# A residual added by TensorE: identity products into the sums' banks, last products by tokens, and squares and last scaling read from PSUM

## The chip, the cores and the metric

One core of a Trainium2 chip runs the whole layer as one program. The metric is the device time in microseconds, the median of several executions. The engines are TensorE (PE: products, with its weight loads as PEld), VectorE (DVE), ScalarE (ACT), GpSimd (POOL) and SyncE (SP), which issues most of the DMAs.

## The reference, cut to what matters

The input x has 256 tokens of 1024 columns, float32. After two attention mixers, x has been raised by the mixers' output; what follows is the part that the change touches:

```python
    x = x + mixed @ w_out[l]
    h = rmsnorm(x, g_ffn[l])
    x = x + conv_ffn(h, w_up[l], conv_w[l], conv_b[l], w_down[l])
return rmsnorm(x, g_final)          # y * rsqrt(mean(y*y) + 1e-6) * g_final

def conv_ffn(h, w_up, conv_w, conv_b, w_down):
    u, gate = jnp.split(h @ w_up, 2, axis=-1)        # 1024 -> 2816 each
    ...                                              # causal conv of width 3 over tokens: uc
    return (jax.nn.gelu(uc) * gate) @ w_down         # 2816 -> 1024
```

## The kernel before, in words

Weights come in units of 128 x 2048 values: one DMA each into `raw`, then ACT makes the high half `whi` (L128) and DVE the low half `wlo` (L132). A product of float32 quality is three products of such halves (high by high, high by low, low by high); the halves are of a type (float32r) that TensorE takes as one record per product. The units are run through in one loop (L1094), in a fixed order. Each engine executes its own instructions in the order in which the program writes them, and a wait holds up all that is behind it on that engine.

From `NFIRST` on the loop does the feed-forward part. For each of 11 steps j there are two units for `w_up` (256 columns each, sums in PSUM tiles `ps_d` and `ps_o` in turn) and, two steps later, one for `w_down` (`mm_down_part`, L630). The down products keep tokens as the 128 output partitions: the sums are `ffn["y"][t][ch]`, with t the half of the tokens and ch the half of the columns, four banks of 128 x 512: both halves of t = 0 in one tile `ps_s`, those of t = 1 in two tiles `ps_t`. They add up over all 11 steps; the last two steps (NF - 2 and NF - 1) are not run in the loop but by `last`, one block of the output at a time, so that the final norm can begin while others are still summed.

Up to there the residual x is kept transposed (`xT`, columns on partitions), since that is how the mixers leave it. In the loop's round `NFIRST + 1` 16 transposes (L1161) by `ident`, the 128 x 128 identity, bring it into the order of tokens, through `ps_t` and `ps_s`, and four ACT copies (L1164) take it to `X` in SBUF. Just ahead of them `rows_of` (L222) spreads the norm's factors over the partitions by two plain float32 products with `ident`.

`last(t, ch, c0, c1)` runs the 24 (or, for half the columns, 12) products of the last two steps for a block, adds the sums to X on DVE (L1201), takes squares and their sum on ACT (L1206), adds the sum to the running one on POOL (L1207), and multiplies X by `gf`, the final norm's gain, on DVE (L1210). The last quarter takes its squares on DVE (L1203). When both column halves of a t are done, POOL takes the power -0.5 (L1209). `store` scales by it on ACT (L1218), for t = 1 partly on DVE (L1216), and issues the DMA out. The order of the blocks is (0,0), (1,0), (0,1), (1,1) in two quarters of 256 columns; the second of these quarters sums its last two steps in a bank of its own, from `ps_d`, and its earlier steps are added to X at the very beginning (L1222).

Of the kernel before, what the change touches and what calls it, by code (L numbers as in the profile page):

```python
# [14 lines left out]
AF = mybir.ActivationFunctionType  # L15
OP = mybir.AluOpType
# [3 lines left out]
D = 1024  # L20
DFF = 2816
NF = DFF // 256
# [71 lines left out]
def build(ctx, tc, a, out):  # L94
    nc = tc.nc
    V, A, P, T = nc.vector, nc.scalar, nc.gpsimd, nc.tensor
# [7 lines left out]
    def pd(shape, tag="d"):  # L104
        return ps.tile([128] + shape, F32, name="ps_" + tag, tag=tag, bufs=1 if tag == "s" else 2)

    xT = const.tile([128, 8, S], F32, name="xT")
# [3 lines left out]
    ident = const.tile([128, 128], F32, name="ident")  # L111
# [5 lines left out]
    nhalf, inv_d, epsc = cst[:, 0:2], cst[:, 2:3], cst[:, 3:4]  # L117
# [66 lines left out]
    def w3(u, k):  # L184
        n = u.n // k
        return (u.hi[:, u.o:u.o + u.n].rearrange("p (k c) -> p k c", k=k),
                u.lo[:, u.o:u.o + u.n].rearrange("p (k c) -> p k c", k=k))
# [386 lines left out]
    ffn = {}  # L574
# [44 lines left out]
    def mm_down_part(u, j, tcs, c0=0, c1=512, own=None):  # L619

        wh, wl = w3(u, 2)
        h, l = ffn["a", j]
        half = [(0, 256), (256, 512)] if c1 - c0 == 512 else [(c0, c1)]
        start, seen = j == (0 if own is None else NF - 2), set()
        for n, (w, x) in enumerate(((wh, h), (wh, l), (wl, h))):
            for t in sorted({t for t, _ in tcs}):
                for kt in range(2):
                    for ch in [ch for q, ch in tcs if q == t]:
                        for b, e in half:
                            T.matmul(ffn["y"][t][ch][:, b:e] if own is None else own, x[:, kt, t * 128:t * 128 + 128],  # L630
                                     w[:, kt, ch * 512 + b:ch * 512 + e], start=start and (t, ch) not in seen,
                                     stop=j == NF - 1 and n == 2 and kt == 1, skip_group_check=True)
                            seen.add((t, ch))

    def mm_down(j):
        def f(u):
            if j == 0:
                s2 = pd([2, 512], "s")
                ta = pd([512], "t")
                tb = pd([512], "t")  # L640
                ffn["y"] = [[s2[:, 0], s2[:, 1]], [ta, tb]]
            if j < NF - 2:
                mm_down_part(u, j, [(t, ch) for t in range(2) for ch in range(2)])
        return f
# [15 lines left out]
    downs = [Unit(2048, mm_down(j)) for j in range(NF)]  # L660
# [353 lines left out]
    def load_to(n):  # L1014
        nonlocal loaded
        while loaded < min(n, len(units)):
            load_unit(units[loaded])
            loaded += 1
# [4 lines left out]
    for n, f in zip(CHUNKS, first):  # L1023
        w = f.shape[-1]
# [32 lines left out]
    for n in CHUNKS:  # L1057
# [6 lines left out]
        for v, u in enumerate((u0, u1)):  # L1064
            r = f[:, :, 256 + 256 * v:512 + 256 * v]
# [24 lines left out]
    def at(i):  # L1090
        return items.get(i, [])

    post = []
    for i, u in enumerate(units):  # L1094
        load_to(i + LA)
        if i == 9:
            cmp_sum()
        for it in at(i - 3):
            it.fin()
        for it in at(i - 2):  # L1100
            it.te()
        for it in at(i - 1):
            it.sm()
        if i == 10:
            cmp_gelu()
        if i == 2:
            hi_of(3)
            lo_of(3)
        if i == 9:
            for it in at(i - 1):  # L1110
                it.sm2()
        if i > 2:
            lo_of(i + 1)
        if i != 9:
            for it in at(i - 1):
                it.sm2()
        if i == 14:
            nc.sync.dma_start(xT, a["xT"])
        if i == 3:
            hi_of(5)  # L1120
            mixer_tiles()
            xc_tile()
            split_cmp(0)
            split_cmp(1)
            u1.evac(u1)
        if i == 4:
            split_keys()
        if i == 11:
            cmp_kv_ev()
        if i == 14:  # L1130

            ob = att.tile([128, 4, S], F32R, name="ob", tag="qa")
            OB.update(h=ob[:, 0:2], l=ob[:, 2:4])
        if i in (23, 24):
            m = ML[i - 23]
            A.activation(m, m, AF.Sigmoid)
        if i == NFIRST:
            st.close()
            ffn["pool"] = ctx.enter_context(tc.tile_pool(name="ffn", bufs=1))
            gf = ffn["pool"].tile([128, D], F32, name="gf")  # L1140
            nc.scalar.dma_start(gf, bass.AP(tensor=a["g_final"].tensor, offset=a["g_final"].offset,
                                            ap=[[0, 128], [1, D]]))
            X = ffn["pool"].tile([128, 2, D], F32, name="X")
            sq = ffn["pool"].tile([128, 512], F32, name="sq")
        if 24 <= i <= 25:
            hi_of(i + 2)
        if i in (24, NFIRST + 2):
            rt["kick"] = "own"
        u.mm(u)
        if not 24 <= i <= 26 and i > 1 and i != 3:  # L1150
            hi_of(i + 2)
        if i == 2:
            u0.evac(u0)
        if i == NFIRST + 1:
            rt["R2"] = rows_of(rt["rs2"], "R2", "o")
            units[NFIRST].evac(units[NFIRST])
            ps2 = pd([2, 512], "s")
            pt = [pd([512], "t"), pd([512], "t"), ps2[:, 0], ps2[:, 1]]
            for q in range(4):
                for c in range(4):  # L1160
                    T.transpose(pt[q][:, c * 128:c * 128 + 128], xT[:, 4 * (q % 2) + c, q // 2 * 128:q // 2 * 128 + 128],  # L1161
                                ident)
            for q in range(4):
                A.activation(X[:, q // 2, q % 2 * 512:q % 2 * 512 + 512], pt[q], AF.Copy)  # L1164
        if post:
            post.pop()()
        if u.pre:
            u.pre(u)
        if u.evac and i not in (0, 1, NFIRST):
            u.evac(u)  # L1170
        if i in (6, 7):
            q_parts(i - 6)
        if i == 7:
            gates_of()
        if u.pre:
            post.append(post_g(len([q for q in units[:i] if q.pre])))
        for it in at(i - 2):
            it.pv()
        for it in at(i - 1):
            it.tr()  # L1180
        for it in at(i):
            it.qk()
        if i == 9:
            cmp_fold()
        if i == 10:
            cmp_kv()


    ss3, rs3 = tiny[:, 6:11], tiny[:, 11:13]

    def last(t, ch, c0=0, c1=512):

        xs, y = X[:, t, ch * 512 + c0:ch * 512 + c1], ffn["y"][t][ch][:, c0:c1]
        w = c1 - c0
        if c0:
            y = pd([512])[:, :w]
        for j in (NF - 2, NF - 1):
            mm_down_part(downs[j], j, [(t, ch)], c0, c1, y if c0 else None)
        n = {(0, 0): 0, (1, 0): 1, (0, 1): 2, (1, 1): 3}[t, ch] + (c0 > 0)
        ss, r = ss3[:, n:n + 1], rs3[:, t:t + 1]  # L1200
        V.tensor_tensor(out=xs, in0=xs, in1=y, op=OP.add)  # L1201
        if c0:
            V.tensor_tensor_reduce(out=sq[:, w:2 * w], in0=xs, in1=xs, scale=1.0 / D, scalar=r,  # L1203
                                   op0=OP.mult, op1=OP.add, accum_out=ss)
        else:
            A.activation(sq[:, :w], xs, AF.Square, scale=1.0 / 32, accum_out=ss)  # L1206
            P.tensor_tensor(out=r, in0=r if ch else epsc, in1=ss, op=OP.add)  # L1207
        if ch and (c0 or t == 0):
            P.tensor_tensor(out=r, in0=ss if c0 else r, in1=nhalf[:, 0:1], op=OP.pow)  # L1209
        V.tensor_tensor(out=xs, in0=xs, in1=gf[:, ch * 512 + c0:ch * 512 + c1], op=OP.mult)  # L1210

    def store(t, c):

        o, r = out[0, t * 128:(t + 1) * 128], rs3[:, t:t + 1]
        if c < D:
            V.tensor_scalar(X[:, t, c:], X[:, t, c:], r, None, op0=OP.mult)  # L1216
            nc.sync.dma_start(o[:, c:], X[:, t, c:])
        A.activation(X[:, t, :c], X[:, t, :c], AF.Copy, scale=r)  # L1218
        (nc.scalar if t else nc.sync).dma_start(o[:, :c], X[:, t, :c])

    x = X[:, 1, 768:1024]
    V.tensor_tensor(out=x, in0=x, in1=ffn["y"][1][1][:, 256:512], op=OP.add)  # L1222
    last(0, 0)
    last(1, 0)
    last(0, 1)
    last(1, 1, 0, 256)
    store(0, D)
    last(1, 1, 256, 512)
    store(1, 384)


# [18 lines left out]
```

## Time and profile before

| | us |
|---|---|
| median of 3 runs (406.04 to 407.66) | 406.07 |
| the profiled execution | 406.5 |
| its span | 404.7 |
| TensorE busy in it | 394.7 |
| DVE busy | 291.2 |
| ACT busy | 212.4 |
| POOL busy | 31.2 |

The times of rows below are counted from the start of the profiled span. A row of the timeline has the start, the duration of the group, engine, line and operation, what is written from what, and the count. A bracket at its end is the idle time of the engine just before, and what ended it. Ends of products are modelled; their starts are not.

### The profile page before, as it was taken

The page shows a single profiled execution, that of the slowest core. Times are in us where ns is not written, and L with a number is a line of the kernel's source. Part 1 is how long each engine was busy: PE and PEld are TensorE (multiplying, and loading weights), DVE is VectorE, ACT ScalarE, POOL GpSimd, SP SyncE. Part 2 cuts the span into 40 slices and gives each one's busy share as a digit, 9 for nine tenths or more (in the row PEclk, how much of TensorE's full clock was granted, in tenths as well). Part 3 has the DMA queues.
Part 4 walks back from the last instruction along what each step waited for, and adds up shares of the span by engine and source line. Part 5 has one row for each costly group of instructions (what it writes and reads, how often), then busy time and mean ns, then how long its engine had stood idle before and what let it go on. Part 6 is the DMA issues. An engine that isn't in the chain of part 4 may idle for free.

```text
span 404.7 us, 8015 instructions
## 1 busy us (share of the span) xinstructions
PE 394.7 (98%) x3412; PEld 383.2 (95%) x3412; DVE 291.2 (72%) x486; ACT 212.4 (52%) x293; POOL 31.2 (8%) x58
## 2 busy tenths in 40 slices
PE   8999989999999999999999999999999999999993
PEld 6999989999998989999999999999999999999992
DVE  5879889887786557458897499676594774946853
ACT  5776764366664345663554765445264352643512
POOL 7100000000000000061143000000000000000012
PEclk9999999999999999999999999999999999999997
DMA  8965746345332532343556346662734726438002
GB/s 319 390 251 207 249 168 209 105 158 220 144 105 105 201 113 105 131 181 108 206 208 235 130 136 236 255 222 108 296 119 194 266 99 261 160 152 299 15 0 105
DMA packets 10980, 72.59 MB, mean 179 GB/s; under 512 B 1216, under 2 KB 1472, under 8 KB 2880
## 3 DMA queue, kind: packets, MB, share of 16 engines
q1 hardware_dynamic: 10512, 70.96, 48.2%
q10 hardware_dynamic: 432, 1.11, 0.7%
q8 instruction: 27, 0.44, 0.4%
q14 instruction: 9, 0.07, 0.1%
HBM read 71.02 MB, written 1.05 MB: 178 GB/s over the span
## 4 chain that ended last, share of the span: by engine, by line
PE 83%; DVE 10%; ACT 2%; DMA 2%; issue 1%; SPq 0%; POOLq 0%; POOL 0%; ACTq 0%
PE ps_d L177 25%; PE ps_d L182 12%; PE ps_o L177 9%; PE ps_s L630 8%; PE ps_t L630 7%; PE ps_o L182 5%; DVE wlo L132 4%; DMA first<-in_first_dram 2%; PE ps_t L177 2%; DVE hTl L202 2%; PE ps_d L344 2%; PE ps_o L905 2%; PE ps_s L946 1%; PE ps_t L892 1%; PE ps_d L280 1%
## 5 line engine op out<-in xcount | busy, mean ns | idle before, releaser
L132 DVE TENSOR_TENSOR wlo<-raw,whi 128x2048 fp32r<-128x2048 f32 (+2 forms) x61 | 135.2, 2217 | 4.2 <-ACT whi L128 4.2
L128 ACT ACTIVATE whi<-raw 128x2048 fp32r<-128x2048 f32 (+1 forms) x61 | 114.8, 1883 | 33.6 <-DMA raw<-in_wts_dram 28.8
L177 PE MATMUL ps_d<-hTh,whi 128*128 128x256 f32 x384 | 90.1, 280 | 0.0
L177 PE MATMUL ps_d<-hTl,whi 128*128 128x256 f32 x384 | 89.0, 277 | 0.0
L177 PEld LDWEIGHTS ps_d<-hTh,whi 128*128 128x128 f32 x384 | 72.2, 188 | 1.7 <-issue 1.3
L177 PEld LDWEIGHTS ps_d<-hTl,whi 128*128 128x128 f32 x384 | 72.2, 188 | 0.0
L182 PE MATMUL ps_d<-hTh,wlo 128*128 128x256 f32 x384 | 47.8, 277 | 0.0
L182 PEld LDWEIGHTS ps_d<-hTh,wlo 128*128 128x128 f32 x384 | 45.7, 188 | 0.0
L177 PE MATMUL ps_o<-hTh,whi 128*128 128x256 f32 x160 | 36.9, 277 | 0.0
L177 PE MATMUL ps_o<-hTl,whi 128*128 128x256 f32 x160 | 36.8, 276 | 0.0
L585 ACT ACTIVATE C<-U,small 128x256 f32<-128x256 f32 x22 | 12.0, 595 | 44.1 <-DVE U L581 44.1
L177 PEld LDWEIGHTS ps_o<-hTl,whi 128*128 128x128 f32 x160 | 30.1, 188 | 0.0
L177 PEld LDWEIGHTS ps_o<-hTh,whi 128*128 128x128 f32 x160 | 30.0, 188 | 0.0
L589 DVE SCALAR_TENSOR_TENSOR C<-U,small,C 128x256 f32<-128x256 f32 x44 | 19.4, 482 | 7.5 <-ACT C L585 7.4
L869 ACT ACTIVATE E<-E,ast 128x256 f32<-128x256 f32 (+1 forms) x32 | 14.2, 444 | 13.4 <-DVE ast L864 13.4
L581 DVE TENSOR_TENSOR U<-ps_d,R 128x512 f32<-128x512 f32 x6 | 4.1, 690 | 23.0 <-PE ps_d L182 19.2
L182 PE MATMUL ps_o<-hTh,wlo 128*128 128x256 f32 x160 | 19.8, 276 | 0.0
L132 POOL TENSOR_TENSOR wlo<-raw,whi 128x1024 fp32r<-128x1024 f32 x3 | 7.7, 2579 | 154.8 <-ACT whi L128 154.8
L182 PEld LDWEIGHTS ps_o<-hTh,wlo 128*128 128x128 f32 x160 | 18.9, 188 | 0.0
L581 DVE TENSOR_TENSOR U<-ps_o,R 128x512 f32<-128x512 f32 x5 | 3.4, 689 | 17.6 <-PE ps_o L182 17.6
L1207 POOL TENSOR_TENSOR tiny<-cst,tiny 128x1 f32<-128x1 f32 x2 | 1.4, 696 | 170.6 <-ACT sq L1206 170.6
L366 DVE TENSOR_TENSOR ML<-ps_d,R 128x512 f32<-128x512 f32 x8 | 5.5, 692 | 12.3 <-PE ps_d L182 12.3
(269 smaller groups left out, 762.5 us busy)
## 6 DMA issues: line engine op xcount, KB each, us to landing
raw<-in_wts_dram SPq DMA_DIRECT2D x61, 1024.0 KB, 4.8
first<-in_first_dram SPq DMA_DIRECT2D x2, 768.0 KB, 8.1
raw<-in_wts_dram SPq DMA_DIRECT2D x1, 1120.0 KB, 11.0
xn<-in_xn_dram SPq DMA_DIRECT2D x2, 512.0 KB, 12.4
xT<-in_xT_dram SPq DMA_DIRECT2D x1, 1024.0 KB, 6.9
first<-in_first_dram SPq DMA_DIRECT2D x2, 384.0 KB, 5.3
gf<-in_g_final_dram ACTq DMA_DIRECT2D x1, 512.0 KB, 3.7
out_dram<-X SPq DMA_DIRECT2D x1, 512.0 KB, 2.6
```

The costliest lines, as they stand in the source:

```text
L128: A.activation(u.hi[:, u.o + c0:u.o + c1], u.raw[:, c0:c1], AF.Copy)
L132: (eng or V).tensor_sub(u.lo[:, u.o + c0:u.o + c1], u.raw[:, c0:c1], u.hi.bitcast(F32)[:, u.o + c0:u.o + c1])
L177: T.matmul(po, l, r, start=start and bank not in banks, stop=False, skip_group_check=True)
L182: T.matmul(po, l, r, start=False, stop=stop and n == len(ks) - 1, skip_group_check=True)
L202: V.scalar_tensor_tensor(hTl[:, kt], x, g[:, kt:kt + 1], hTh.bitcast(F32)[:, kt], op0=OP.mult, op1=OP.subtract)
L344: T.matmul(u.p[:, i], l[:, kt, i * 128:i * 128 + 128], r[:, kt], start=kt == 0 and i == 0 and q == 0, stop=kt == 7 and q == 2, skip_group_ ...
L581: V.tensor_tensor(out=U[:, :, 2:], in0=u.p, in1=bc(rt["R2"], 2), op=OP.mult)
L585: A.activation(C[:, c], U[:, c, 2:], AF.Identity, scale=CW(2, t), bias=CB[:, t:t + 1])
L589: V.scalar_tensor_tensor(C[:, c], U[:, c, w:w + S], CW(w, t), C[:, c], op0=OP.mult, op1=OP.add)
L630: T.matmul(ffn["y"][t][ch][:, b:e] if own is None else own, x[:, kt, t * 128:t * 128 + 128], w[:, kt, ch * 512 + b:ch * 512 + e], start=st ...
L869: A.activation(self.E[:, i], self.E[:, i], AF.Exp, bias=mn[:, i:i + 1], scale=-1.0, accum_out=dn[:, i:i + 1])
L905: T.matmul(oA[js[c]][g * 64:g * 64 + 64, t * 128:(t + 1) * 128], Vn[:, k, b * 128 + g * 64:b * 128 + g * 64 + 64], self.PT[:, i], start=t ...
```

## The change

The four banks of the sums are now taken in round `NFIRST + 1`, and instead of 16 transposes 16 plain float32 products of the tiles of `xT` with `ident` write the residual into them: the first of each bank clears it, the other three write their own columns. All down products then add to it, and the four ACT copies into X go away. `last` goes by tokens: (0,0), (0,1), then the scaling and the store of t = 0, then (1,0) and the two quarters of (1,1). ACT takes the squares directly from the bank, DVE multiplies bank by `gf` into X. Now the first quarter of (1,1) has the bank of its own: its earlier sums are copied to X by ACT at the beginning (L1208 of the changed kernel), and DVE adds. For the last quarter ACT takes the squares from the bank, DVE adds their sum to the running one (L1201), POOL takes the power, and one DVE instruction multiplies bank, factor and `gf` (L1217). ACT scales 512 columns of t = 1 and DVE 256 more, which are 512 with those of L1217; each half has its store.

```diff
-        start, seen = j == (0 if own is None else NF - 2), set()
+        start, seen = own is not None and j == NF - 2, set()
...
         if i == NFIRST + 1:
             rt["R2"] = rows_of(rt["rs2"], "R2", "o")
             units[NFIRST].evac(units[NFIRST])
-            ps2 = pd([2, 512], "s")
-            pt = [pd([512], "t"), pd([512], "t"), ps2[:, 0], ps2[:, 1]]
-            for q in range(4):
-                for c in range(4):
-                    T.transpose(pt[q][:, c * 128:c * 128 + 128], xT[:, 4 * (q % 2) + c, q // 2 * 128:q // 2 * 128 + 128],
-                                ident)
-            for q in range(4):
-                A.activation(X[:, q // 2, q % 2 * 512:q % 2 * 512 + 512], pt[q], AF.Copy)
+
+            s2 = pd([2, 512], "s")
+            ta = pd([512], "t")
+            tb = pd([512], "t")
+            ffn["y"] = [[s2[:, 0], s2[:, 1]], [ta, tb]]
+            for t in range(2):
+                for ch in range(2):
+                    for c in range(4):
+                        T.matmul(ffn["y"][t][ch][:, c * 128:c * 128 + 128], xT[:, 4 * ch + c, t * 128:t * 128 + 128],
+                                 ident, start=c == 0, stop=False, skip_group_check=True)
...
-        if c0:
-            y = pd([512])[:, :w]
+        own = pd([512])[:, :w] if c1 == 256 else None
         for j in (NF - 2, NF - 1):
-            mm_down_part(downs[j], j, [(t, ch)], c0, c1, y if c0 else None)
+            mm_down_part(downs[j], j, [(t, ch)], c0, c1, own)
         n = {(0, 0): 0, (1, 0): 1, (0, 1): 2, (1, 1): 3}[t, ch] + (c0 > 0)
         ss, r = ss3[:, n:n + 1], rs3[:, t:t + 1]
-        V.tensor_tensor(out=xs, in0=xs, in1=y, op=OP.add)
-        if c0:
-            V.tensor_tensor_reduce(out=sq[:, w:2 * w], in0=xs, in1=xs, scale=1.0 / D, scalar=r,
-                                   op0=OP.mult, op1=OP.add, accum_out=ss)
-        else:
-            A.activation(sq[:, :w], xs, AF.Square, scale=1.0 / 32, accum_out=ss)
-            P.tensor_tensor(out=r, in0=r if ch else epsc, in1=ss, op=OP.add)
+        if own is not None:
+            V.tensor_tensor(out=xs, in0=xs, in1=own, op=OP.add)
+            y = xs
+        A.activation(sq[:, :w], y, AF.Square, scale=1.0 / 32, accum_out=ss)
+        (V if c0 else P).tensor_tensor(out=r, in0=r if ch else epsc, in1=ss, op=OP.add)
         if ch and (c0 or t == 0):
-            P.tensor_tensor(out=r, in0=ss if c0 else r, in1=nhalf[:, 0:1], op=OP.pow)
-        V.tensor_tensor(out=xs, in0=xs, in1=gf[:, ch * 512 + c0:ch * 512 + c1], op=OP.mult)
...
+            P.tensor_tensor(out=r, in0=r, in1=nhalf[:, 0:1], op=OP.pow)
+        if not c0:
+            V.tensor_tensor(out=xs, in0=y, in1=gf[:, ch * 512 + c0:ch * 512 + c1], op=OP.mult)
+
+
+    A.activation(X[:, 1, 512:768], ffn["y"][1][1][:, 0:256], AF.Copy)
     last(0, 0)
+    last(0, 1)
+    A.activation(X[:, 0], X[:, 0], AF.Copy, scale=rs3[:, 0:1])
+    nc.sync.dma_start(out[0, 0:128], X[:, 0])
     last(1, 0)
-    last(0, 1)
     last(1, 1, 0, 256)
-    store(0, D)
     last(1, 1, 256, 512)
-    store(1, 384)
+    o, r = out[0, 128:256], rs3[:, 1:2]
+    V.scalar_tensor_tensor(X[:, 1, 768:], ffn["y"][1][1][:, 256:512], r, gf[:, 768:], op0=OP.mult, op1=OP.mult)
+    V.tensor_scalar(X[:, 1, 512:768], X[:, 1, 512:768], r, None, op0=OP.mult)
+    nc.sync.dma_start(o[:, 512:], X[:, 1, 512:])
+    A.activation(X[:, 1, :512], X[:, 1, :512], AF.Copy, scale=r)
+    nc.scalar.dma_start(o[:, :512], X[:, 1, :512])
```

How this moves the instructions is seen best on the two engines that take turns behind the last products. On ACT, from the first squares to the end of the program, there stood before (`sq,tiny<-X` are squares and their sum, `X<-X,tiny` a scaling by the norm's factor):

```order
L1206 ACTIVATE sq,tiny<-X 128x512 [waits DVE_49]
L1206 ACTIVATE sq,tiny<-X 128x512 [waits DVE_49,Activation_49] x2
L1206 ACTIVATE sq,tiny<-X 128x256 [waits DVE_49,Activation_49]
L1218 ACTIVATE X<-X,tiny 128x1024 [waits Pool_49]
L1218 ACTIVATE X<-X,tiny 128x384 [waits Pool_49]
L1219 DMA out_dram<-X 128x384 [waits Activation_49]
```

And in the changed kernel, on the same engine and in the same place:

```order
L1208 ACTIVATE X<-ps_t 128x256 [waits PE_49]
L1200 ACTIVATE sq,tiny<-ps_s 128x512 [waits PE_49]
L1200 ACTIVATE sq,tiny<-ps_s 128x512 [waits DVE_49,PE_49]
L1211 ACTIVATE X<-X,tiny 128x1024 [waits DVE_49,Pool_49]
L1200 ACTIVATE sq,tiny<-ps_t 128x512 [waits PE_49,Activation_49]
L1200 ACTIVATE sq,tiny<-X 128x256 [waits DVE_49,Activation_49]
L1200 ACTIVATE sq,tiny<-ps_t 128x256 [waits PE_49,Activation_49]
L1220 ACTIVATE X<-X,tiny 128x512 [waits Pool_49]
```

The squares wait for TensorE instead of DVE, the scaling of 1024 columns has moved from behind all of ACT's squares to between those of t = 0 and those of t = 1, and the last quarter's squares are ACT's. On DVE, the same stretch before (`X<-X,ps_s` is the addition of sums to X, `X<-X,gf` the product with the gain; the two rows of ISA are squares with their sum and the read of that sum):

```order
L1222 TENSOR_TENSOR X<-X,ps_t 128x256 [waits PE_49]
L1201 TENSOR_TENSOR X<-X,ps_s 128x512 [waits PE_49]
...
L1210 TENSOR_TENSOR X<-X,gf 128x512 [waits Activation_49]
L1201 TENSOR_TENSOR X<-X,ps_t 128x256 [waits PE_49]
L1210 TENSOR_TENSOR X<-X,gf 128x256 [waits Activation_49]
L1201 TENSOR_TENSOR X<-X,ps_d 128x256 [waits PE_49]
L1203 ISA sq,tiny<-X,tiny 128x256 [waits DVE_49,Pool_49]
L1203 ISA tiny 128x1
L1210 TENSOR_TENSOR X<-X,gf 128x256 [waits DVE_49]
L1216 TENSOR_SCALAR X<-X,tiny 128x640 [waits DVE_49,Pool_49]
```

And in the changed kernel:

```order
L1205 TENSOR_TENSOR X<-ps_s,gf 128x512 [waits Activation_49] x2
L1205 TENSOR_TENSOR X<-ps_t,gf 128x512 [waits Activation_49]
L1198 TENSOR_TENSOR X<-X,ps_d 128x256 [waits PE_49]
L1205 TENSOR_TENSOR X<-X,gf 128x256 [waits Activation_49]
L1201 TENSOR_TENSOR tiny<-tiny 128x1 [waits Activation_49,Pool_49]
L1217 SCALAR_TENSOR_TENSOR X<-ps_t,tiny,gf 128x256 [waits Pool_49]
L1218 TENSOR_SCALAR X<-X,tiny 128x256 [waits DVE_49]
```

Four of five additions of sums are gone from DVE, the products with the gain read the banks and wait for ACT's squares of the same bank, and what is left for DVE behind the last product is the addition of one column ahead of POOL's power, and two instructions behind it.

## Rows read from the trace of the kernel before

**Rows 1.** Busy time by stretch: start:end, its length, then busy of each engine (instructions).

```profile
core 0: us, PE busy (x) PEld busy (x) DVE busy (x) ACT busy (x) POOL busy (x), PEclk, DMA share, GB/s
...
300.00:350.00 50.00, 50.00 (x437) 50.00 (x437) 33.24 (x37) 23.36 (x21) 0.00 (x0) 1.00 0.53 194
```

**Rows 2.** Waits from 216 us on: who, for whom, total, times, longest.

```profile
PEld ps_d L280 <- DVE wlo L132: 0.6, 1, 0.6
```

**Rows 3.** Timeline of the weight loads: start, duration, line, operation, stationary size, count.

```profile
65.23 0.85 PEld L905 LDWEIGHTS ps_o<-PT,Vn 128*64 128x64 f32 x16
...
223.95 0.53 PEld L222 LDWEIGHTS ps_o<-ident,tiny 128*128 128x128 f32 x4
224.40 0.91 PEld L1161 LDWEIGHTS ps_t<-ident,xT 128*128 128x128 f32 x8
...
226.15 0.19 PEld L172 LDWEIGHTS ps_o<-hTh,whi 128*128 128x128 f32 x1
```

**Rows 4.** Groups by line and shape, TensorE: shape, count, busy us, mean ns.

```profile
L222 PE MATMUL ps_o<-ident,tiny 128*128 128x128 f32 x8 | 1.2, 274 | 0.0
```

**Rows 5.** The chain that ended last, at the last down products: start, duration, what.

```profile
392.05 2.84 PE ps_s L630 x24
...
394.92 0.70 DVE X L1201
```

**Rows 6.** Timeline of all engines from the last quarter's products to the last store.

```profile
396.56 0.63 POOL L1207 TENSOR_TENSOR tiny<-tiny 128x1 f32<-128x1 f32 x1 [2.20 <-ACT sq L1206]
...
397.28 0.55 POOL L1209 TENSOR_TENSOR tiny<-tiny,cst 128x1 f32<-128x1 f32 x1
397.31 0.40 PE L630 MATMUL ps_d<-wlo,ah 128*128 128x256 f32 x2
397.57 0.42 ACT L1206 ACTIVATE sq<-X 128x256 f32<-128x256 f32 x1 [1.15 <-DVE X L1201]
397.89 0.19 ACT L1206 ACTIVATION_READ_ACCUMULATOR sq<-X 128x1 f32 x1
397.99 1.13 ACT L1218 ACTIVATE X<-X,tiny 128x1024 f32<-128x1024 f32 x1
398.11 0.42 DVE L1210 TENSOR_TENSOR X<-X,gf 128x256 f32<-128x256 f32 x1 [0.64 <-ACT sq L1206]
...
398.45 0.41 DVE L1201 TENSOR_TENSOR X<-X,ps_d 128x256 f32<-128x256 f32 x1
399.02 0.48 DVE L1203 CUSTOM_DVE_ANT_0 sq<-X,tiny 128x256 f32<-128x256 f32 x1 [0.15 <-DVE X L1201]
...
399.59 0.79 POOL L1209 TENSOR_TENSOR tiny<-tiny,cst 128x1 f32<-128x1 f32 x1 [1.00 <-DVE tiny L1203]
400.41 0.61 ACT L1218 ACTIVATE X<-X,tiny 128x384 f32<-128x384 f32 x1 [1.29 <-POOL tiny L1209]
...
401.06 0.36 ACTq L1219 DMA_DIRECT2D out_dram<-X  x1
```

**Rows 7.** Groups by line and shape, ACT and DVE: count, busy us, mean ns.

```profile
L1164 ACT ACTIVATE X<-ps_s 128x512 f32<-128x512 f32 x2 | 1.1, 595 | 0.0
L917 ACT ACTIVATE oah<-ps_o 128x256 fp32r<-128x256 f32 x4 | 1.3, 381 | 4.3 <-PE ps_o L910 4.3
...
L1210 DVE TENSOR_TENSOR X<-X,gf 128x512 f32<-128x512 f32 x3 | 2.1, 693 | 2.5 <-ACT sq L1206 2.5
L964 DVE TENSOR_SCALAR ast<-ast 128x1 f32<-128x1 f32 x4 | 0.6, 147 | 0.0
L454 DVE SCALAR_TENSOR_TENSOR qb<-ps_d,scB,R 128x256 f32<-128x256 f32 x6 | 2.6, 479 | 1.0 <-PE ps_d L182 1.0
L883 DVE TENSOR_SCALAR E<-E,ast 128x256 f32<-128x256 f32 x16 | 4.6, 350 | 0.1
```

**Rows 8.** The last two stores: DMA issues by line with size and us to landing.

```profile
out_dram<-X SPq DMA_DIRECT2D x1, 320.0 KB, 2.4
out_dram<-X ACTq DMA_DIRECT2D x1, 192.0 KB, 2.6
```

More of the change, by code (lines that the diff above doesn't have):

```diff
@@ L636, in f @@
         def f(u):
[L637 to L641, printed above, removed]
             if j < NF - 2:
@@ L1208, in last @@
-        if ch and (c0 or t == 0):
-            P.tensor_tensor(out=r, in0=ss if c0 else r, in1=nhalf[:, 0:1], op=OP.pow)
-        V.tensor_tensor(out=xs, in0=xs, in1=gf[:, ch * 512 + c0:ch * 512 + c1], op=OP.mult)
[L1212 to L1219, printed above, removed]
@@ L1221, in build @@
-    x = X[:, 1, 768:1024]
-    V.tensor_tensor(out=x, in0=x, in1=ffn["y"][1][1][:, 256:512], op=OP.add)
+        if own is not None:
[3 more added lines that the diff above has]
+        (V if c0 else P).tensor_tensor(out=r, in0=r if ch else epsc, in1=ss, op=OP.add)
+        if ch and (c0 or t == 0):
+            P.tensor_tensor(out=r, in0=r, in1=nhalf[:, 0:1], op=OP.pow)
+        if not c0:
+            V.tensor_tensor(out=xs, in0=y, in1=gf[:, ch * 512 + c0:ch * 512 + c1], op=OP.mult)
```

## The prediction

> **What bounds the kernel now.** I read first the busy time by stretch, then the waits, then the weight loads around the removed transposes, and last the end of the program row by row. In the stretch from 300 to 350 us TensorE is busy for 50.00 of 50.00 us and its weight loads too, at a granted clock of 1.00, which is the 2.4 GHz level, while DVE has 33.24 and ACT 23.36 [rows 1]. From 216 us to the end the only thing that TensorE's queue waits for is one low half of a weight, 0.6 us [rows 2], and that is before the transposes. They run from 224.40 to 226.15 us, closed in by weight loads on both sides without a gap [rows 3]. So from there to its last product TensorE sets the time: what is added to it moves the end by as much, and what is taken from DVE or ACT in that part moves nothing. After the last product, which ends at 397.31 + 0.40 = 397.71 us [rows 6], a chain over DVE, POOL and ACT sets the end. I call this moment E. The two ends are separate sums, since nothing that TensorE does after E matters and nothing of the last chain begins before the last products do.
>
> **The identity products.** The change puts 16 products of xT with the identity, float32 on both sides, where 16 transposes of the same tiles stood. The 16 transposes (eight into one tile, eight more into the next) took 226.15 - 224.40 = 1.75 us [rows 3], 0.109 us each. A float32 product is not one record but two: the program's two row-spreading products just before give 4 records (it calls that helper twice with two products, and the trace has 8 in all [rows 4]), and those 4 took 224.40 - 223.95 = 0.45 us [rows 3], so 0.225 us a product. They have the same shape, 128x128 stationary and 128 columns of the identity moving. 16 x 0.225 = 3.60 us, so TensorE gets 3.60 - 1.75 = **1.85 us** longer. Bounds: the products with only 64 stationary columns and the same 128 moving ones took 0.85 us for 16 records, 0.053 each [rows 3]; if that were the pace, 32 records would be 1.70 us and the change -0.05. At the pace of the down products, 2.84 us for 24 [rows 5], 0.118 each, 32 records are 3.79 and the change +2.04. I take 1.85, since its row has both sizes right and the lower one has half of the weight columns.
>
> The Trainium skill (TensorE: Matmul & The Clock Gate, section Terms) says that a transpose mode is 4x faster for float32; by that 16 products would be 4 x 1.75 = 7.0 us and the addition 5.25 us instead of 1.85. The trace does not agree so far: its float32 product costs 0.225 us against 0.109 for a transpose, 2.1x [rows 3].
>
> **What goes for nothing.** Four ACT copies of 128x512 (0.6 us each [rows 7]) leave the stretch behind the transposes, and DVE loses the early addition into X. Both stand beside a TensorE that doesn't wait, so I give them 0. The first down products no longer clear their banks, which changes a flag and no duration. The new early copy of half a bank (ACT, 0.38 us by the row of that size from PSUM [rows 7]) is ready when the third last down step is done; the last product into that bank half follows 10 us later, so 0.
>
> **The last products by tokens.** Their count and sizes stay: 24 products of 256 columns take 2.84 us [rows 5], 12 take 1.42. With the new order the blocks end at E - 5.68 (tokens 0, right half), E - 2.84 (tokens 1, left), E - 1.42 (first quarter of the last block) and E. What must be weighed is ACT's queue: the scaling of all 1024 columns of tokens 0 (1.13 us [rows 6]), with a wait for POOL and DVE, now stands ahead of the squares of tokens 1, left. Behind it are queued three squares, and the sum for the end waits for each. Its time: squares of 512 columns from E - 5.65, 0.60 from PSUM [rows 7] and 0.19 for the read of the sum [rows 6], to E - 4.86; POOL 0.08 later, the addition 0.63 or less and the power 0.55 [rows 6], to about E - 3.57; the scaling to E - 2.41, so that the next squares begin 0.4 us late; 0.79 for them, to E - 1.59; DVE's product with gf may read the bank only behind them, 0.69 [rows 7], to E - 0.87; the addition of the quarter, 0.41 and overlapped by 0.08, to E - 0.54; its squares, 0.32 + 0.19 [rows 6], to E + 0.01. The last squares could begin at E + 0.03 at the earliest. So the early scaling costs nothing, but with a cover of 0.02 us only.
>
> **The end.** Before, DVE stood at E + 0.03 behind the product with gf, which waited for ACT: the addition began at 398.45, that is E + 0.74 instead of E + 0.03, the squares on DVE ended at 399.50, POOL's power at 400.38, ACT's last scaling at 401.02 and its store was issued at 401.06, E + 3.35 [rows 6]. After: squares straight from the bank at E + 0.03 (a product's end to its reader: 392.05 + 2.84 to 394.92 [rows 5]), about 0.29 and 0.19 (256 columns from PSUM are 0.381 against 0.42 from X, so 0.32 shrinks by some 0.03 [rows 6, 7]), to E + 0.51; DVE's addition of one column, 0.15 [rows 7], to E + 0.69; POOL 0.08 later with the power, 0.79 [rows 6], to E + 1.56. Then two engines end together. ACT scales 512 columns: between 0.61 for 384 and 1.13 for 1024 [rows 6] that is 0.72, to E + 2.31, store at E + 2.35. DVE has the product with r and gf from PSUM, 0.48, and the scaling of 256 columns, 0.35 [rows 7], overlapped by 0.08, to E + 2.34, store at E + 2.38. The last issue is thus **0.97 us** earlier after E. The stores took 2.4 and 2.6 us with 320 and 192 KB [rows 8]; two of 256 KB move the same bytes, so 0. Bounds: with the shorter power (0.55) the gain is 1.21; with the power for tokens 0 at 0.79 too, ACT's queue runs 0.24 late up to the last squares, which begin 0.22 later, and the gain is 0.75.
>
> **The sum.** The profiled execution took 406.5 us, its span 404.7: 406.5 + 1.85 - 0.97 = 407.4. It lies 0.4 above the median of the runs, 406.07, so for the median: 406.07 + 0.88 = **407.0 us**. The bounds of both terms give 406.07 - 0.05 - 1.21 = 404.8 and 406.07 + 2.04 - 0.75 = 407.4.
>
> **Rivals.** (a) *The products cost what the transposes did.* Then only the end counts: 406.07 - 0.97 = 405.1. For it: 0.053 us a record where the weights have 64 columns. Against: two records a product and 0.112 us each in the row of the same shape [rows 3]. (b) *The products cost four transposes*, and the end is on the slower side. Place: TensorE between the row-spreading products and the first product of the next block; price 5.25 us, so 406.07 + 5.25 - 0.97 = 410.3. It decides from 0.30 us a product on: there 16 x 0.30 = 4.80 is 3.05 above the transposes, and with the end's gain the sum passes 0.5%. The rule named above would have it; for it, too, is that the shown float32 products have a stationary side that is one column repeated. Against it is their row. (c) *ACT's queue holds the end up.* The early scaling has a cover of 0.02 us. If DVE's product with gf and the scaling each come late by a POOL step (0.55 to 0.79 us [rows 6]), the last squares begin that much behind E and the gain is gone: 406.07 + 1.85 - 0.1 = 407.8.
>
> **How the numbers follow.** Forecast 0.74, (a) 0.07, (b) 0.07, (c) 0.12. The range: 405.9 to 408.2. It takes in the forecast with both bounds of the end and the upper one of the products, and (c), with 0.4 for the scatter between profile and median; it leaves out (a) and (b) and a few hundredths of the rest. A measurement can tell some 0.5% of this kernel, 2.0 us, from no change: 404.0 to 408.1. Faster than that needs (a) with more besides: 0.03. Slower is (b) and a little of (c): 0.10. Same: 0.87.
>
> **What would show it.** Right: 32 float32 records where 16 transposes stood, some 3.6 us long, with no gap before the next block; TensorE's last product some 1.85 us later; the last store's issue 2.4 us behind it, where it was 3.35; ACT's last squares at once behind the last product. Wrong: 1.8 or 7 us of identity products; a gap on TensorE beyond them; last squares that begin over 0.3 us behind the last product, with ACT's scaling or DVE's product with gf in front of them; a power on POOL of another length than 0.55 to 0.79.

## The result and the profile after

The changed kernel takes 408.81 us (median of 8 runs; 406.11 us for the kernel before in the same rounds). The ratio is 1.0065, with a 95% interval of 1.0055 to 1.0074, so it is 2.2 to 3.0 us slower. The forecast was 407.0 us, no change that can be told, in a range that ended at 408.2.

The profiled execution itself took 410.11 us (span 408.2), 1.3 above the median of its kernel. The busy time by stretch shows where that comes from, long before the changed code runs; first the kernel before, then the changed one (columns as in [rows 1]):

```profile
58.00:62.00 4.00, 3.94 (x32) 3.68 (x33) 3.98 (x6) 1.09 (x3) 0.00 (x0) 1.00 0.21 27
```

```profile
58.00:62.00 4.00, 4.00 (x23) 3.79 (x23) 3.93 (x7) 0.82 (x2) 0.00 (x0) 0.65 0.20 45
```

The granted clock was 0.65 there, a mean between its two levels of 1.2 and 2.4 GHz, and TensorE got 23 products done instead of 32. By the row-spreading products this execution is 1.1 us behind the one of before. So I compare only lengths from there on. The chain that ended last, at those products (what [rows 3] show as weight loads); first before, then after:

```profile
224.68 0.87 PE ps_t L1161 x8
225.55 0.87 PE ps_s L1161 x8
226.42 0.03 PE ps_o L172
...
386.40 2.83 PE ps_s L630 x24
```

```profile
225.36 0.44 PE ps_o L222 x4
225.80 1.79 PE ps_s L1160 x16
227.59 1.79 PE ps_t L1160 x16
229.37 0.03 PE ps_o L172
```

The identity products are 32 records in 3.58 us, where the transposes had 16 in 1.74. The next block follows without a gap. From 229.37 to the first product of the first output block at 389.35, 159.98 us pass; before, the same way (226.42 to 386.40) took 159.98 us too. There the two kernels part, as the chain shows again (the view of [rows 5]):

```profile
389.35 2.84 PE ps_s L630 x24
392.19 0.02 issue
392.21 0.70 ACT sq L1200 x2
392.91 0.02 issue
392.93 0.70 DVE X L1205
393.63 0.04 issue
393.68 3.02 PE ps_s L630 x24
```

Between the first block (tokens 0, left half) and the second (tokens 0, right half), TensorE leaves the chain: ACT's squares and DVE's product with gf stand in it. The waits from 216 us on have two rows that the kernel before doesn't have (who, for whom, total, times, longest):

```profile
PEld ps_s L630 <- DVE X L1205: 1.7, 1, 1.7
PE ps_s L630 <- DVE X L1205: 1.5, 1, 1.5
```

TensorE sat idle for 1.5 us. The end of the program, in the timeline of all engines (the view of [rows 6]):

```profile
401.74 0.39 PE L630 MATMUL ps_t<-wlo,ah 128*128 128x256 f32 x2
401.88 0.42 DVE L1205 TENSOR_TENSOR X<-X,gf 128x256 f32<-128x256 f32 x1 [0.64 <-ACT sq L1200]
401.99 0.36 POOL L1201 TENSOR_TENSOR tiny<-tiny 128x1 f32<-128x1 f32 x1 [1.53 <-ACT sq L1200]
402.22 0.38 ACT L1200 ACTIVATE sq<-ps_t 128x256 f32<-128x256 f32 x1 [0.38 <-PE ps_t L630]
402.50 0.19 ACT L1200 ACTIVATION_READ_ACCUMULATOR sq<-ps_t 128x1 f32 x1
402.80 0.16 DVE L1201 TENSOR_TENSOR tiny<-tiny 128x1 f32<-128x1 f32 x1 [0.50 <-ACT sq L1200]
403.04 0.55 POOL L1203 TENSOR_TENSOR tiny<-tiny,cst 128x1 f32<-128x1 f32 x1 [0.69 <-DVE tiny L1201]
403.62 0.72 ACT L1220 ACTIVATE X<-X,tiny 128x512 f32<-128x512 f32 x1 [0.93 <-POOL tiny L1203]
403.62 0.48 DVE L1217 SCALAR_TENSOR_TENSOR X<-ps_t,tiny,gf 128x256 f32<-128x256 f32 x1 [0.67 <-POOL tiny L1203]
404.02 0.34 DVE L1218 TENSOR_SCALAR X<-X,tiny 128x256 f32<-128x256 f32 x1
404.40 0.34 SPq L1219 DMA_DIRECT2D out_dram<-X  x1
```

The last product ends at E = 402.13 and the last store is issued at 404.40, E + 2.27 instead of E + 3.35. The stores (size and time to landing, as in [rows 8]) take a little longer than the 2.4 and 2.6 us of before:

```profile
out_dram<-X ACTq DMA_DIRECT2D x1, 256.0 KB, 2.8
out_dram<-X SPq DMA_DIRECT2D x1, 256.0 KB, 2.5
```

From the last issue to the end of the span 3.80 us pass instead of 3.64. The account of the two profiles: 3.58 - 1.74 = 1.84 for the products; from the first product of `last` to E 402.13 - 389.35 = 12.78 against 397.71 - 386.40 = 11.31, 1.47 net for the idle time; -1.08 for the end; 0.16 for the stores (spans are printed to 0.1 us, so this term is known to about that). The sum is 2.39, within the 2.2 to 3.0 that the runs give.

### The profile page after: what moved, and what is told of

The parts are those of the page before. It is cut to its first block, busy times and chain, and to the rows that moved or that the text cites. A ratio compares the mean times of both kernels' runs of the same rounds, so it can differ in the third digit from the quotient of the medians.

```text
span 408.2 us, 8041 instructions
## 1 busy us (share of the span) xinstructions
PE 397.8 (97%) x3428; PEld 386.3 (95%) x3428; DVE 288.0 (71%) x480; ACT 211.1 (52%) x292; POOL 29.5 (7%) x58
## 4 chain that ended last, share of the span: by engine, by line
PE 84%; DVE 10%; ACT 3%; issue 1%; DMA 1%; POOL 0%; POOLq 0%; DVEq 0%; ACTq 0%
PE ps_d L177 25%; PE ps_d L182 12%; PE ps_o L177 9%; PE ps_s L630 8%; PE ps_t L630 6%; PE ps_o L182 5%; DVE wlo L132 4%; PE ps_d L344 3%; PE ps_t L177 2%; DVE hTl L202 2%; PE ps_o L900 2%; PE ps_s L941 1%; PE ps_t L887 1%; PE ps_d L280 1%; PE ps_o L995 1%; PE ps_t L970 1%
## 5 line engine op out<-in xcount | busy, mean ns | idle before, releaser
L177 PE MATMUL ps_d<-hTh,whi 128*128 128x256 f32 x384 | 91.6, 283 | 0.0
L177 PE MATMUL ps_d<-hTl,whi 128*128 128x256 f32 x384 | 90.4, 280 | 0.0
L177 PEld LDWEIGHTS ps_d<-hTh,whi 128*128 128x128 f32 x384 | 73.3, 191 | 1.7 <-issue 1.3
L177 PEld LDWEIGHTS ps_d<-hTl,whi 128*128 128x128 f32 x384 | 73.4, 191 | 0.0
L630 PE MATMUL ps_s<-whi,ah 128*128 128x256 f32 x88 | 12.5, 282 | 1.5 <-DVE X L1205 1.5
```

The source lines that it names most:

```text
L177: T.matmul(po, l, r, start=start and bank not in banks, stop=False, skip_group_check=True)
```

## The experiments

The theory after this reading had three parts: the identity products cost two records each where a transpose has one; the idle time comes from the tile `ps_s`, which holds the banks of both halves of tokens 0, so that products into one bank wait for all reads of the other; the end is worth 1 us. The rivals were that the wait would only move elsewhere, that the products were innocent, and that the end's gain hung on TensorE's delay.

**The banks apart.** The left half of tokens 1 shares the tile with the left half of tokens 0; the right half of tokens 0 has a tile of its own:

```diff
-            ffn["y"] = [[s2[:, 0], s2[:, 1]], [ta, tb]]
+            ffn["y"] = [[s2[:, 0], ta], [s2[:, 1], tb]]
```

> The changed kernel with one edit: of the tile ps_s, which has two banks, the second now holds the left half of tokens 1, and the right half of tokens 0 lies in a ps_t tile. Theory A (the changed kernel's products of the right half of tokens 0 wait until ACT and DVE have read the left half, because both lie in one tile: 1.50 us of idle TensorE in its trace): the idle time goes, and the time falls by 1.2 to 1.5 us against the changed kernel, to 1.0 to 1.5 above the kernel before (about 407.3). Rival B (the wait only stands where another would: the reads of the banks are slow, and the end of the program waits for them anyhow): TensorE's idle time goes but ACT's queue ends as late as before, so 0 to 0.4 less than the changed kernel, about 408.5.

Measured: 407.05 us, ratio to the kernel before 1.0027 (1.0017 to 1.0037), so 1.1 above it, where the change was 2.6 above: 1.5 us less. The chain of this kernel at the same place:

```profile
387.84 2.83 PE ps_s L630 x24
390.66 2.84 PE ps_t L630 x24
393.50 0.02 issue
```

The second block follows the first at once. Theory A holds, in the size too; nothing else in the end took the wait's place: the last store is issued at E + 2.28, as late behind the last product as in the changed kernel.

**Transposes into the banks.** The 16 identity products become float32 transposes:

```diff
                     T.matmul(ffn["y"][t][ch][:, c * 128:c * 128 + 128], xT[:, 4 * ch + c, t * 128:t * 128 + 128],
-                                 ident, start=c == 0, stop=False, skip_group_check=True)
+                                 ident, is_transpose=True, start=c == 0, stop=False, skip_group_check=True)
```

> The changed kernel with one edit: the 16 identity products are issued as float32 transposes, one record each, into the same banks, the first of a bank clearing it and the others not; the down products add to them as before. Theory A (a float32 product is two records where a transpose is one, 0.112 us each): 1.8 us less than the changed kernel, about 0.8 above the kernel before (406.9). Rival B (the products cost no more than the transposes, and the whole loss is in the last part): 0 less, about 408.7. Rival C (adding to a bank that is filled early slows the down products): also 0 less.

Measured: 406.67 us, ratio 1.0018 (1.0009 to 1.0027): 0.7 above the kernel before, 1.9 less than the change. Theory A holds. The chain of this kernel has 16 records again:

```profile
224.11 0.87 PE ps_s L1160 x8
224.99 0.87 PE ps_t L1160 x8
```

A transpose can fill a bank that products then add to, and it costs half. TensorE's wait of 1.5 us at the second block is still there in this kernel.

**Both edits.**

> Both edits together: the banks of tokens 0 in different tiles, and float32 transposes instead of identity products. Theory A: the gain of the end alone is left, some 1.0 us below the kernel before, about 405.1, ratio 0.9975. If the two losses overlap, or if the gain of the end hangs on the idle time (TensorE late, so ACT and DVE are free earlier): 405.5 to 406.1, no gain.

Measured: 405.25 us, ratio 0.9985 (0.9973 to 0.9998): 0.1 to 1.1 us faster than the kernel before. The two losses add up: 1.5 and 1.9 us are 0.8 more than the 2.6 that the change lost, and with both gone a gain is left. The interval holds the 1.0 us expected and much smaller gains too, so its size is taken from the trace: the last product ends at 397.87 + 0.40 = 398.27 and the last store is issued at 400.54, E + 2.27 as in the changed kernel. So the end's gain doesn't hang on TensorE's delay.

```profile
397.40 0.42 ACT L1200 ACTIVATE sq<-X 128x256 f32<-128x256 f32 x1 [1.18 <-DVE X L1198]
...
397.73 0.18 ACT L1200 ACTIVATION_READ_ACCUMULATOR sq<-X 128x1 f32 x1
397.87 0.40 PE L630 MATMUL ps_t<-wlo,ah 128*128 128x256 f32 x2
...
398.36 0.38 ACT L1200 ACTIVATE sq<-ps_t 128x256 f32<-128x256 f32 x1 [0.45 <-PE ps_t L630]
...
400.54 0.34 SPq L1219 DMA_DIRECT2D out_dram<-X  x1
```

ACT is idle for 0.45 us ahead of the last squares: its queue does have cover here.

**The products alone.** In the kernel before, products in place of the transposes, into the same temporary tiles:

```diff
-                    T.transpose(pt[q][:, c * 128:c * 128 + 128], xT[:, 4 * (q % 2) + c, q // 2 * 128:q // 2 * 128 + 128],
-                                ident)
+                    T.matmul(pt[q][:, c * 128:c * 128 + 128], xT[:, 4 * (q % 2) + c, q // 2 * 128:q // 2 * 128 + 128],
+                             ident, start=True, stop=True)
```

> The kernel before with one edit: the 16 transposes are plain float32 products with the identity, into the same temporary tiles, with the same four ACT copies. This is the price of the products alone. Theory A: 32 records, 3.6 us in place of 1.75, and the time rises by 1.8 to 1.9 us, to about 408.0. Rival B (no dearer than transposes): no change. Rival C (four transposes each): 5.2 us, about 411.3.

Measured: 407.94 us, ratio 1.0046 (1.0034 to 1.0059), 1.4 to 2.4 us. The line's instructions (count, then duration in ns least/median/most, first and last start):

```profile
L1161 PE MATMUL ps_t<-ident,xT x16: 275/275/276, 224.1 to 225.8; 128*128 128x128 f32 x16
L1161 PE MATMUL ps_s<-ident,xT x16: 275/275/276, 225.9 to 227.6; 128*128 128x128 f32 x16
```

16 products are 32 records, 0.112 us apart. Theory A holds, as forecast.

**The order alone.** The kernel before, with its additions to X and its transposes, but the blocks by tokens:

```diff
     last(0, 0)
-    last(1, 0)
     last(0, 1)
+    last(1, 0)
```

> The kernel before with one edit: the last products by tokens, (0,0), (0,1), (1,0), (1,1), all else as it was (transposes into temporary tiles, additions to X on DVE). Theory A (the wait comes from the order together with the tile of two banks, not from the reads by ACT): the products of (0,1) now wait until DVE has added (0,0), some 0.7 us of idle TensorE where the changed kernel had 1.5 behind two readers, and the time rises by 0.5 to 0.8 us, to about 406.6. Rival (the wait needs the reads of PSUM by ACT): no idle TensorE, no change, 406.0.

Measured: 406.98 us, ratio 1.0027 (1.0016 to 1.0038), 0.6 to 1.5 us. The chain shows the same break with one reader instead of two:

```profile
385.93 2.84 PE ps_s L630 x24
388.77 0.02 issue
388.80 0.70 DVE X L1201
389.50 0.04 issue
389.54 3.01 PE ps_s L630 x24
```

So the wait needs the order and, by the first experiment, the shared tile, and no read by ACT. The kernel before had the same tile, but between the two halves of tokens 0 it ran the 24 products of tokens 1, 2.83 us, and the read was over by then: DVE's addition ended at 389.95, and the next products into `ps_s` began at 391.89. With ACT's squares ahead of DVE's product the wait doubles, which is what the change has.

**ACT's queue.** The kernel with both edits, and 0.6 us more on ACT behind the early scaling:

```diff
     A.activation(X[:, 0], X[:, 0], AF.Copy, scale=rs3[:, 0:1])
+    A.activation(sq, X[:, 0, 0:512], AF.Copy)
```

> The kernel with both repairs (banks apart, transposes) and one more ACT instruction, a copy of 512 columns, 0.6 us, right behind the early scaling of tokens 0; its result is not used. Theory A (ACT's queue has no cover left: the last squares begin 0.07 us after they could): the last squares begin some 0.6 us later, and the time rises by 0.5 to 0.6, to about 405.8. Rival (the queue has room, the end follows TensorE): under 0.15 more, about 405.3.

Measured: 405.35 us, ratio 0.9984 (0.9971 to 0.9996), the same as without (0.9985): the rival's figure, but with intervals of 1 us the runs can't tell 0.3 us from nothing. In its timeline the last product ends at 398.36 + 0.40 = 398.76:

```profile
398.36 0.40 PE L630 MATMUL ps_t<-wlo,ah 128*128 128x256 f32 x2
...
399.11 0.38 ACT L1200 ACTIVATE sq<-ps_t 128x256 f32<-128x256 f32 x1
...
401.29 0.34 SPq L1220 DMA_DIRECT2D out_dram<-X  x1
```

The last squares begin at E + 0.35 instead of E + 0.09, the last store is issued at E + 2.53 instead of E + 2.27. Of 0.63 us added, 0.26 came through in the trace. By it neither theory had it quite right: ACT's queue has a cover, against theory A, but it is some 0.4 us and doesn't hide everything.

**The old end.** The kernel with both edits, but the last quarter as before:

```diff
-        own = pd([512])[:, :w] if c1 == 256 else None
+        own = pd([512])[:, :w] if c0 else None
...
         if own is not None:
             V.tensor_tensor(out=xs, in0=xs, in1=own, op=OP.add)
             y = xs
+            V.tensor_tensor_reduce(out=sq[:, w:2 * w], in0=xs, in1=xs, scale=1.0 / D, scalar=r,
+                                   op0=OP.mult, op1=OP.add, accum_out=ss)
...
-    A.activation(X[:, 1, 512:768], ffn["y"][1][1][:, 0:256], AF.Copy)
+    A.activation(X[:, 1, 768:1024], ffn["y"][1][1][:, 256:512], AF.Copy)
     last(0, 0)
     last(0, 1)
-    A.activation(X[:, 0], X[:, 0], AF.Copy, scale=rs3[:, 0:1])
-    nc.sync.dma_start(out[0, 0:128], X[:, 0])
     last(1, 0)
     last(1, 1, 0, 256)
+    store(0, D)
     last(1, 1, 256, 512)
...
+    store(1, 384)
```

> The kernel with both repairs, but with the end of the kernel before for the last quarter: a bank of its own for it, the addition and the squares on DVE, scaling and store of tokens 0 behind the first quarter, 640 and 384 columns in the last stores. What is left of the change are the residual in the banks and ACT's squares from PSUM for the other blocks. Theory A (the gain is that of the last quarter, 1.07 us from the last product to the last store's issue): the gain goes, about 406.0, as the kernel before. Rival (the residual in the banks alone shortens the end): it stays, 405.3.

Measured: 405.38 us, ratio 0.9982 (0.9973 to 0.9990), as fast as with the new last quarter. The rival holds. The timeline:

```profile
396.53 0.42 DVE L1207 TENSOR_TENSOR X<-ps_t,gf 128x256 f32<-128x256 f32 x1 [0.52 <-ACT sq L1203]
...
396.94 0.40 PE L630 MATMUL ps_d<-wlo,ah 128*128 128x256 f32 x2
397.37 0.42 DVE L1198 TENSOR_TENSOR X<-X,ps_d 128x256 f32<-128x256 f32 x1 [0.42 <-PE ps_d L630]
...
399.99 0.36 ACTq L1215 DMA_DIRECT2D out_dram<-X  x1
```

The last product ends at 397.34, DVE's addition begins at once, and the last store is issued at E + 2.65. So 0.70 of the 1.08 us come without the new last quarter. They come from the first quarter: its squares and its product with gf now read the bank, need no addition first, and are through (396.53 + 0.42 = 396.95) when the last product ends. In [rows 6] that product with gf stood in DVE's queue from 398.11 on, 0.4 us behind the last product, with the last addition behind it. The order is not the cause: with it alone the last store was issued at 401.45, 3.46 us behind a last product that ended at 397.99. The new last quarter itself brings 0.38 us in the traces (0.24 of it because POOL's last power takes 0.55 us instead of 0.79), and the two stores of 256 KB take 0.16 of it back; the runs can't tell the rest from nothing.

## Why the prediction was wrong, point by point

- **What bounds the kernel.** Right: from the transposes to the last product TensorE's additions moved the end one for one, as far as the runs can tell, and the 159.98 us between didn't change when four ACT copies went.
- **The identity products.** Right, 1.85 forecast: 1.84 in the trace, 1.9 by the products alone, 1.9 by their removal. The lower bound (the pace of 64 stationary columns) and the rule of the Trainium skill (TensorE: Matmul & The Clock Gate, section Terms), 4x, were both off: the traces have 2.1x.
- **The last products by tokens: the step that failed.** It let the blocks end 2.84 us apart, "Their count and sizes stay", and then weighed ACT's queue alone. It asked of each reader whether its input is late, but not of TensorE whether its output may be written. Both halves of tokens 0 lay in the one tile `ps_s`; with the new order the second half's products follow while ACT and DVE still read the first, where before another block stood between. Worked out from the rows at hand the wait would have been 0.60 - 0.10 + 0.19 for the squares and the read of their sum, which overlap by 0.10 [rows 6], 0.69 for the product with gf and three hand-overs of some 0.03, about 1.5 us, which is what came (1.50 idle, 1.47 net). That term is what the sum lacked: 407.0 + 1.5 = 408.5. The 0.3 us that are left to the measured time are within the interval of the runs.
- **ACT's queue** in the same step: the cover of 0.02 us was mis-sized. It was about 0.4. POOL's addition ahead of the power took 0.19 where [rows 6] had 0.63, squares with the read of their sum took 0.70 instead of 0.79, and the last squares waited for the last product alone.
- **The end.** Its size was near, 0.97 forecast and 1.08 measured to the last issue, in part by luck: the last power took 0.55 instead of the 0.79 put into the sum, and the steps ahead of it were 0.14 later than forecast (POOL's power began at E + 0.91, not E + 0.77). The largest part was named rightly: DVE's queue held the last addition up by 0.71 us (E + 0.74 instead of E + 0.03). What frees it was not: I gave that to the new last quarter, whose squares need no addition, and 0.70 of the gain is there without it, since the first quarter is done earlier. The stores, for which I gave 0, cost 0.16.
- **The rivals.** None of the three came: the products were neither as cheap as transposes (a) nor at four of them (b), and ACT's queue (c) did not hold the end. The loss was a wait of TensorE, named under "What would show it" as a gap, but given neither a place nor a price.

## What to carry to other kernels

When blocks of output change their order, follow each product's output, not only its inputs: which reads of that tile, in any of its banks, are still to come, and how long the work between was that hid them. A wait that is always met costs nothing and stands in the order all the same; it is the first thing that a new order can bring to life. A float32 transpose can start a sum in a bank just as a product with the identity can, at one record instead of two.

## What the runs showed of the hardware that was not expected

How long POOL's addition of one column takes goes with what DVE does beside it. First a row of before, beside DVE's product of X with gf, both in SBUF, from 398.11 to 398.53 [rows 6]; then two of the changed kernel, where that product reads a bank:

```profile
398.16 0.43 POOL L1207 TENSOR_TENSOR tiny<-tiny 128x1 f32<-128x1 f32 x1 [0.33 <-ACT sq L1206]
```

```profile
397.44 0.69 DVE L1205 TENSOR_TENSOR X<-ps_s,gf 128x512 f32<-128x512 f32 x1 [3.82 <-ACT sq L1200]
397.55 0.19 POOL L1201 TENSOR_TENSOR tiny<-tiny 128x1 f32<-128x1 f32 x1 [4.38 <-ACT sq L1200]
```

Before, the addition ended at 398.59, 0.06 us behind DVE; three others beside 0.69 us of the same product took 0.63 to 0.70. After, beside a product of a bank with gf, the same additions took 0.19. The one beside 401.88, where DVE again reads X and gf, took 0.36 and ended at 402.35, 0.05 behind DVE. The last power goes the same way: 0.79 in the kernel before and in the one with the old end, where a product of X with gf begins 0.05 us ahead of it, and 0.55 in the changed kernel, where DVE does nothing beside it. The Trainium skill (SBUF — State Buffer, section Who interferes with whom) says that a DVE instruction with two inputs in SBUF contends with a GpSimd one that reads SBUF, and that one with at most one input there, outside DVE's two-port modes, doesn't. These rows agree. No experiment was made for it alone.

Down products of the same size follow each other every 0.118 us up to the idle time (2.84 for 24), and every 0.114 behind it (in the order-alone kernel 2.73 for the 24 into `ps_t`). In the kernels without the idle time all run at 0.118. No run looked for the cause.
